# A latent attention stage with its maxima taken in eight portions, its row vectors made by one transposition, and its column sums taken an item later

## The chip, the cores and the metric

The kernel runs on one core of one Trainium2 chip. The metric is device time in microseconds (us) of one execution of the whole program. The core has a matrix engine (TensorE, PE in the profile, with its weight loads as PEld), three engines for elementwise work and reductions (VectorE is DVE, ScalarE is ACT, GpSimd is POOL), and SyncE (SP), which here does nothing but issue transfers between the chip's main memory (DRAM) and the on-chip memory, one after the other. Matmul results land in eight PSUM banks, which this program names bs (three of them), bm (three) and bv (two).

## The reference

One layer over 1024 latent and 256 context tokens of width 1024: a half-step SwiGLU block, two attentions in parallel (neighbourhood attention, and latent attention, MLA, with eight heads), a gated merge, and a second half-step SwiGLU block. The change touches the latent attention alone:

```python
def _attend(q, k, v):
    s = jnp.einsum('bqhd,bkhd->bhqk', q * q.shape[-1] ** -0.5, k).astype(jnp.float32)
    p = jax.nn.softmax(s, axis=-1).astype(v.dtype)
    return jnp.einsum('bhqk,bkhd->bqhd', p, v)
...
q_mla = _mla_q(qn, _axial_rope(qr, ang_r, ang_c))
k_mla = jnp.concatenate([k_ctx_mla, _mla_k(kn, _axial_rope(kr, ang_r, ang_c))], axis=1)
v_mla = jnp.concatenate([cvb, vb], axis=1)
o_mla = _blocked_attention(q_mla, k_mla, v_mla)
```

Each head has 1024 queries and 1280 keys (256 context, 1024 latent). A softmax row needs a shift that is near its maximum, and the sum of its exponentials.

## The kernel before

The work of the latent attention is cut into 16 **items**: item i is head i // 2 and 512 of its queries (the even item the first 512, the odd one the rest). Keys are in ten blocks of 128, two to a step, so an item has five **score steps** p = 0 to 4. A step is ten matmuls: five terms of a product in split precision for each of two key blocks, which sit in the upper and the lower half of the 128 partitions. The scores stand with keys in partitions and queries in columns, so the shift has to be a **row** (one number for each column). It is written as row 32 of each half in the second 512 columns of a query tile (`q[..][1]`, qb below) and enters the scores with the fifth term. ACT then makes the exponentials of both blocks (`Exp`).

Before an item's scores, its shift is made. `maxima` is a generator of **units**: each unit makes coarse scores with queries in partitions, and DVE reduces them to their maxima. An item has five units: four of 512 keys (one for each 128 queries, for both halves of the keys), and a fifth of the remaining 128 keys for all four. `shift` reduces these to four columns of 128 numbers, and `row` turns them into rows: PE multiplies each column, broadcast, with an identity matrix, and ACT copies four pieces of 256 numbers from PSUM into the query tile.

After its scores, an item is **weighed** (`weigh`): 20 matmuls multiply the exponentials with the values, eight matmuls with a column of ones make the column sums (over `l`, in which POOL and DVE have added up the ten blocks), DVE takes their inverses, PE turns these into rows as in `row`, and `out` copies the rows from PSUM, multiplies, and stores both parts of the split result (`heads_out`).

The order is written out by hand in `follow(i, p)`, which is called after score step p of item i. In step 0 it makes the shift of item i + 1 and weighs item i - 1; in the midst of that weighing stands `row` of item i + 1. Units are taken one to a step, so that the fifth unit of item i + 1 comes in step 0 of item i, ahead of the shift. Every engine works through its list in the order of the program.

Loads go through SP, one instruction each, in the order of the program too. The tiles of a head are loaded in four groups: `queries(0)`, ten loads, and the leading keys, six (`leading`, in step 0 of an odd item i, for head i // 2 + 2); then the rest of the keys, eight, and `queries(1)`, ten (`first`), and three loads of values (`second`), both in step 1 of an even item, for head i // 2 + 1. That is 37 loads to a head. An SP instruction that has to wait (for a tile to come free, or for data to store) holds up all that are behind it.

Of the kernel before, what the change touches and what calls it, by code (L numbers as in the profile page):

```python
# [15 lines left out]
P = 128  # L16
# [22 lines left out]
def f32(ap):  # L39
    return ap.bitcast(F32)  # L40
# [3 lines left out]
def hybrid_block(ctx: ExitStack, tc: tile.TileContext, a: dict, out: bass.AP):  # L44
# [1718 lines left out]
    def heads_out(o, free, b, views, cast=False):  # L1763


        for s in range(2):
# [7 lines left out]
            nc.gpsimd.tensor_tensor(lo[b:b + 64], x, f32(hi[b:b + 64]), op=ALU.subtract)  # L1774
# [136 lines left out]
    class MlaHead:  # L1911
# [5 lines left out]
        def leading(self):  # L1917
            self.queries(0)
            self.k1, self.k2 = W(), W()
# [65 lines left out]
    far = []  # L1985

# [6 lines left out]
    max_bank = ["m"]  # L1993
    mla_heads = [MlaHead(h) for h in range(NH)]

    class MlaItem:
# [6 lines left out]
        def maxima(self):  # L2003
# [4 lines left out]
            def products(pb, t, x, keys):  # L2008
# [3 lines left out]
                for u, (q, k) in enumerate(((qa, hd.k1), (qb, hd.k2))):  # L2012
                    for e in range(2):
                        r = slice(64 * e, 64 * e + 64)
                        mmul(pb[e][:, x], q[r, c], k[r, keys], u == 0, u == 1)
                open_group[0] = False

            for t in range(4):
                pb = [PB(max_bank[0]) for _ in range(2)]
                products(pb, t, slice(0, 512), slice(0, 512))  # L2020
                for e in range(2):
                    nc.vector.tensor_reduce(d[:, t, e:e + 1], pb[e], axis=AX.X, op=ALU.max)  # L2022
                yield
            pb = [PB(max_bank[0]) for _ in range(2)]
            for t in range(4):
                products(pb, t, slice(t * P, (t + 1) * P), slice(512, 640))
            for e in range(2):
                nc.vector.tensor_reduce(d[:, :, 2 + e], pb[e].rearrange("p (t c) -> p t c", t=4), axis=AX.X, op=ALU.max)  # L2028
            yield

        def shift(self):


            self.n_ = ST(4)
# [10 lines left out]
        def scores(self, p):  # L2045
            hd = self.hd
            qa, qb = hd.q[self.i % 2]
            pb = [PB("s"), PB("v" if (5 * self.i + p) % 2 else "s")]
            lo, hi, k = slice(0, 512), slice(512, 1024), slice(p * P, (p + 1) * P)
            open_group[0] = True  # L2050
            for u in range(5):
                for e in range(2):
                    r = slice(64 * e, 64 * e + 64)
                    x, y = ((hd.k1[r, k], qa[r, lo]), (hd.k1[r, k], qa[r, hi]), (hd.low_keys(r, p), qa[r, lo]),
                            (hd.k2[r, k], qb[r, lo]), (hd.k3[r, k], qb[r, hi]))[u]
                    mmul(pb[e], x, y, u == 0, u == 4)
            open_group[0] = False
            for e in range(2):
# [3 lines left out]
                nc.scalar.activation(self.part(kb), pb[e], AF.Exp)  # L2062
# [4 lines left out]
        def add(self, kb):  # L2067


            p, n = self.part(kb), 8 if self.i < 14 else 4  # L2070
# [13 lines left out]
        def finish(self):  # L2084
            self.add(8)
            self.add(9)
            nc.vector.tensor_tensor(self.l, self.l, self.acc, op=ALU.add)  # L2087

        def weigh(self):
            self.pv = pv = PB("v")  # L2090
            r, t = ST(4), T2()
            self.rb, self.o = t[:, 0:256], t[:, 256:512]
            for kb in range(10):
                v = self.hd.value(kb)
                x = self.part(kb)
                weigh(pv, 0, (v, v), (x[:, 0:256], x[:, 256:512]), kb == 0, kb == 9)
            for x in range(4):
                weigh(pv, 256 + x, [self.l[:, x * P + 64 * e:x * P + 64 * e + 64] for e in range(2)], (ones, ones), True, True)
            nc.vector.reciprocal(r, pv[:, 256:260])
            if self.i + 2 < 2 * NH:  # L2100
                mla[self.i + 2].row()
            rows_of(pv, 256, r)

        def out(self):
            h, pv, rb, o = self.hd.h, self.pv, self.rb, self.o
            nc.scalar.copy(rb, pv[:, 256:512])
            nc.vector.tensor_tensor(o, pv[:, 0:256], rb, op=ALU.mult)
# [109 lines left out]
    for n in range(len(todo)):  # L2217
# [5 lines left out]
        if n == len(todo) - 3:  # L2223
            max_bank[0] = "s"
            mla_heads[1].leading()
        ahead = chain(start(EARLY), start(AHEAD)) if n == 0 else start(n + AHEAD) if n + AHEAD < len(todo) else top({len(todo) - 3: 2}.get(n, 1))
# [345 lines left out]
```

## Time and profile before

| | |
|---|---|
| time, median of 3 runs | 2552.16 us (2551.08 to 2552.7) |
| the profiled execution | 2552.3 us, span 2550.5 us |
| PE / PEld / DVE / ACT / POOL busy, share of the span | 98% / 81% / 71% / 45% / 12% |
| granted TensorE clock, mean | 0.998 |
| latent attention, first and last exponentials of line 2062 | begin at 1469.5 and 1737.1 us |
| chain that ended last, by engine | PE 87%, ACT 3%, DVE 3%, POOL 3%, DMA 2%, issue 1%, SPq 1% |

A busy PE is read with care: matmuls are pipelined and their ends are modelled. The queue of SP is shown as SPq; its instructions are only the issue of a transfer, and the time to landing runs from the start of the issue until the data is there. Outside the latent attention and the last few items of the neighbourhood attention just ahead of it (nearly nine tenths of the span) the change moves nothing.

### The profile page before, as it was taken

The numbers are of one execution on the slowest core, as the hardware profiler recorded it, in microseconds if no ns is written. First come the engines' busy times: TensorE is split into PE (matmuls) and PEld (weight loads), VectorE is DVE, ScalarE is ACT, GpSimd is POOL, SyncE is SP. The second block draws the span as 40 slices with busy tenths as digits, with TensorE's granted clock in tenths as the row PEclk, the third lists the DMA queues.
The fourth block names the chain that finished last, engine by engine and source line by source line (L and its number), as shares of the span: only waits on it lengthen the run. The fifth ranks groups of instructions, "written<-read, shape, count | busy, mean of one in ns | idle before, by whom it ended". The sixth has DMA issues, their size and how long they took to land.

```text
span 2550.5 us, 39567 instructions
## 1 busy us (share of the span) xinstructions
PE 2502.7 (98%) x14376; PEld 2075.7 (81%) x14376; DVE 1817.2 (71%) x3101; ACT 1145.5 (45%) x2102; POOL 298.8 (12%) x384
## 2 busy tenths in 40 slices
PE   8999999999999999999999999989999999999998
PEld 6888888888898888889887876667888888888887
DVE  4789996887786577874356655556886888766777
ACT  5632233445654753433446744541366323233444
POOL 1000000000000000001002356661021000000003
PEclk9999999999999999999999999999999999999999
DMA  8455543943674566655879764416845445326724
GB/s 308 154 177 191 200 145 120 334 149 136 220 276 144 205 225 215 209 166 174 227 243 246 210 156 119 116 45 241 317 141 197 161 158 164 113 98 239 268 71 165
DMA packets 271877, 474.57 MB, mean 186 GB/s; under 512 B 62658, under 2 KB 96578, under 8 KB 271684
## 3 DMA queue, kind: packets, MB, share of 16 engines
q1 hardware_dynamic: 271684, 472.06, 56.9%
q8 instruction: 113, 1.85, 0.3%
q14 instruction: 80, 0.66, 0.1%
HBM read 355.35 MB, written 116.59 MB: 185 GB/s over the span
## 4 chain that ended last, share of the span: by engine, by line
PE 87%; ACT 3%; DVE 3%; POOL 3%; DMA 2%; issue 1%; SPq 1%; POOLq 0%; DVEq 0%; ACTq 0%
PE bs L157 37%; PE bm L157 29%; PE bv L157 19%; POOL t L2077 2%; PE bm L160 1%; DMA w<-d 1%; SPq L135 1%; DVE t L2087 1%; PE bs L160 1%; ACT t L123 1%; PE bv L160 1%; ACT xp L2062 1%; DVE kr L2028 1%; DVE xu L123 0%; ACT xu L123 0%
## 5 line engine op out<-in xcount | busy, mean ns | idle before, releaser
L123 ACT CAST xu<-t 128x512 fp32r<-128x512 f32 (+1 forms) x270 | 161.0, 601 | 493.9 <-DVE t L123 351.6
L157 PE MATMUL bm<-xu,xu 128*128 128x512 f32 (+2 forms) x1572 | 366.7, 387 | 0.0
L157 PE MATMUL bs<-xv,xu 128*128 128x512 f32 x1488 | 357.3, 389 | 0.3 <-DVE t L123 0.3
L157 PE MATMUL bv<-xv,xu 128*128 128x512 f32 x1342 | 335.4, 389 | 0.0
L157 PEld LDWEIGHTS bm<-xu,xu 128*128 128x128 f32 x1572 | 288.0, 188 | 56.9 <-issue 0.3
L157 PEld LDWEIGHTS bs<-xv,xu 128*128 128x128 f32 x1488 | 279.2, 188 | 58.9 <-issue 1.1
L157 PEld LDWEIGHTS bv<-xv,xu 128*128 128x128 f32 x1342 | 251.9, 188 | 52.2
L157 PE MATMUL bs<-xv,xv 128*128 128x512 f32 x1086 | 265.8, 390 | 0.0
L123 POOL TENSOR_SCALAR st<-st 128x1 f32<-128x1 f32 (+1 forms) x66 | 33.6, 509 | 1883.6 <-ACT t L123 1865.4
L123 DVE TENSOR_TENSOR xu<-xu,xu 128x512 fp32r<-128x512 f32 (+1 forms) x296 | 201.7, 686 | 73.0 <-ACT xu L123 72.5
L157 PEld LDWEIGHTS bs<-xv,xv 128*128 128x128 f32 x1086 | 203.0, 188 | 41.6
L157 PE MATMUL bs<-xu,xu 128*128 128x512 f32 (+1 forms) x972 | 226.1, 381 | 0.0
L123 DVE TENSOR_TENSOR t<-t,t 128x512 f32<-128x512 f32 (+2 forms) x278 | 185.3, 674 | 45.9 <-ACT t L123 36.6
L157 PEld LDWEIGHTS bs<-xu,xu 128*128 128x128 f32 x972 | 177.4, 188 | 35.6 <-issue 1.4
L123 DVE TENSOR_TENSOR xu<-t,xu 128x512 fp32r<-128x512 f32 (+1 forms) x270 | 179.3, 664 | 10.7 <-ACT xu L123 10.6
L157 PE MATMUL bm<-xv,xv 128*128 128x512 f32 x690 | 182.9, 390 | 0.0
L123 ACT CAST xv<-t 128x512 fp32r<-128x512 f32 x170 | 105.7, 622 | 166.9 <-PE bv L157 69.2
L123 ACT CAST xu<-xu 128x512 fp32r<-128x512 f32 x218 | 132.7, 618 | 70.2 <-DMA xu<-in_wo 57.1
L123 DVE TENSOR_TENSOR xv<-t,xv 128x512 fp32r<-128x512 f32 x170 | 117.1, 689 | 64.2 <-ACT xv L123 63.8
L157 PE MATMUL bs<-w,w 64*128 64x512 f32 (+3 forms) x916 | 157.0, 379 | 1.6 <-DVE kr L2022 0.7
L157 PEld LDWEIGHTS bm<-xv,xv 128*128 128x128 f32 x690 | 129.2, 188 | 27.0 <-issue 0.4
L157 PE MATMUL bm<-t,xu 128*128 128x256 f32 x1224 | 147.9, 283 | 0.0
(263 smaller groups left out, 3971.7 us busy)
## 6 DMA issues: line engine op xcount, KB each, us to landing
d<-t SPq DMA_DIRECT2D x350, 256.0 KB, 2.5
t<-d SPq DMA_DIRECT2D x274, 256.0 KB, 3.8
xu<-in_f1w SPq DMA_DIRECT2D x59, 512.0 KB, 4.2
xu<-in_f2w SPq DMA_DIRECT2D x58, 512.0 KB, 3.8
t<-in_wada SPq DMA_DIRECT2D x112, 256.0 KB, 5.0
xv<-in_f1w SPq DMA_DIRECT2D x44, 512.0 KB, 7.4
xu<-in_winT SPq DMA_DIRECT2D x38, 512.0 KB, 4.4
w<-d SPq DMA_DIRECT2D x66, 256.0 KB, 4.7
```

The source lines that it names most:

```text
L123: return lambda *x, **y: pin(f(*x, **y))
L135: return pin(nc.sync.dma_start(dst, src))
L157: return pin(nc.tensor.matmul(o, s, m, start=start, stop=stop, skip_group_check=open_group[0]))
L160: return pin(nc.tensor.transpose(o, x, i))
L2028: nc.vector.tensor_reduce(d[:, :, 2 + e], pb[e].rearrange("p (t c) -> p t c", t=4), axis=AX.X, op=ALU.max)
L2062: nc.scalar.activation(self.part(kb), pb[e], AF.Exp)
L2077: nc.gpsimd.tensor_tensor(self.acc, self.acc, p, op=ALU.add)
L2087: nc.vector.tensor_tensor(self.l, self.l, self.acc, op=ALU.add)
```

## The change

Four things change, all in the latent attention.

1. **Maxima.** An item's maxima come in eight units, each of 128 queries and 320 keys of each half, where there were four of 512 keys and one of four times 128. The units are taken one to a score step, with steps 2 and 4 cut in two for a second one, and one more at the end of step 0: eight to an item. Sixteen units come before item 0, so that those taken in item i are all of item i + 2: its first before the weighing, seven behind.
2. **Rows.** The shift of item i + 1 and the inverse sums of item i - 2 are put side by side into one tile of eight columns. One transposition by PE makes eight rows of them, one ACT copy takes them out of PSUM, and SP carries them on: eight transfers of one row each into the query tile of item i + 1, and, for the inverse sums (of items 0 to 12), one transfer to DRAM and two from there, which repeat a row over 64 partitions each. This is `to_rows`, in step 0.
3. **Column sums.** For items below FAST = 13 the last sum over blocks moves from DVE to POOL and into step 2 of the next item, the column sums and inverses into step 0 of the item behind that, and `out` into step 1 of item i + 4; the weighed values are copied from PSUM at once. Items 13 to 15 keep the way of before.
4. **Loads.** `queries(0)` is issued in step 3 of an even item, the leading keys in step 0 of an odd item behind the transfers of `to_rows`; `first` and `second` stay in step 1 of even items. An early extra `first` of head 1 goes. The low part in `heads_out` moves from POOL to DVE.

```diff
     def to_rows(i, pb):
+        lo, hi = 0 if i + 1 < 2 * NH else 4, 8 if 0 <= i - 3 < FAST else 4
+        turn_(pb[0:hi - lo, 384:512], columns[i][:, lo:hi], ident)
+        rows = T2()
+        nc.scalar.copy(rows[0:hi - lo, 0:P], pb[0:hi - lo, 384:512])
+        if lo == 0:
+            after = mla[i + 1]
+            for e in range(2):
+                for t in range(4):
+                    put(f32(after.hd.q[after.i % 2][1][64 * e + 32:64 * e + 33, 512 + t * P:640 + t * P]), rows[t:t + 1, 0:P])
+        if hi == 8:
+            d = DR([4, P])
+            put(d, rows[4 - lo:8 - lo, 0:P])
+            for x in range(2):
+                put(mla[i - 3].rb[64 * x:64 * x + 64, :],
+                    d.rearrange("t p -> (t p)")[256 * x:256 * x + 256].partition_broadcast(64))
...
             for t in range(4):
-                pb = [PB(max_bank[0]) for _ in range(2)]
-                products(pb, t, slice(0, 512), slice(0, 512))
-                for e in range(2):
-                    nc.vector.tensor_reduce(d[:, t, e:e + 1], pb[e], axis=AX.X, op=ALU.max)
-                yield
...
+                for x in range(2):
+                    pb = [PB(x) for x in next(max_banks)]
+                    products(pb, t, slice(320 * x, 320 * x + 320))
+                    for e in range(2):
+                        nc.vector.tensor_reduce(d[:, t, 2 * x + e:2 * x + e + 1], pb[e][:, 0:320], axis=AX.X, op=ALU.max)
+                    yield
...
-        if after and p == (0 if i else 2):
-            after.shift()
-        if p == 0 and prev:
+        if p == 0:
+            if after:
+                after.shift()
+            if prev:
+                if i > FAST:
+                    prev.total()
+                prev.weigh()
+            pb = prev.pv if prev else PB("v")
+            if 0 <= i - 2 < FAST:
+                mla[i - 2].sums(pb, columns_of(i + 1)[:, 4:8])
+            to_rows(i, pb)
             if i % 2 and i // 2 + 2 < NH:
-                mla_heads[i // 2 + 2].leading()
-            prev.weigh()
...
+                mla_heads[i // 2 + 2].leading_keys()
...
+        if 0 <= i - 4 < FAST - 1 and p == 1:
+            mla[i - 4].out()
...
+        if p == 3 and i % 2 == 0 and i // 2 + 2 < NH:
+            mla_heads[i // 2 + 2].queries(0)
```

**The order on SP.** First the list of before, from the end of one head's `leading` to the `first` of the next. In all these lists a name is a tile with its buffer's number; here w tiles hold queries and keys, and d tensors are in DRAM.

```order
L135 DMA w_16305<-d_381 32x512
L135 DMA w_16305<-d_387 32x512
L135 DMA w_16316<-d_384 64x5x128 x2
L135 DMA w_16317<-d_386 32x5x128 x4
L135 DMA w_16587<-d_386 32x5x128
L135 DMA w_16587<-d_387 32x640
```

All of it is loads from DRAM, with nothing that another engine computes. Now the same place with the change: leading keys of a head (w_15964, w_15965), then `to_rows` of an even item (t_16154 is its ACT copy, t_15689 the tile of the repeated rows), then `first` of that head, down to its second queries (w_16213, w_16214).

```order
L135 DMA w_15964<-d_383 64x5x128 x2
L135 DMA w_15965<-d_386 32x5x128 x4
L135 DMA w_15772<-t_16154 1x16x8 x8
L135 DMA d_16164<-t_16154 4x128
L135 DMA t_15689<-d_16164 64x256 x2
L135 DMA w_16204<-d_386 32x5x128
L135 DMA w_16204<-d_387 32x640
```

Eleven transfers that come from the ACT copy of this item stand between the leading keys and the rest of the head's loads; the second queries come eight loads further down, and the next head's leading keys stand behind eleven more (of t_16392).

**The order on PE in step 0 of an item.** Before, from the last product of the fifth unit on (bm_16914): weighing into bv_16935, column sums (strip holds the ones), rows of the shift (bm_16967), rows of the inverse sums.

```order
L157 MATMUL bm_16914<-w_16317,w_16597 128x128
L157 MATMUL bv_16935<-xp_16698,w_16165 64x256 x10
L157 MATMUL bv_16935<-xp_16835,w_16165 64x256 x2
L157 MATMUL bv_16935<-xp_16835,w_15895 64x256 x4
L157 MATMUL bv_16935<-xp_16835,y_12989 64x256 x4
L157 MATMUL bv_16935<-strip,t_16910 64x1 x8
L157 MATMUL bm_16967<-ident,st_16933 64x128 x4
L157 MATMUL bv_16935<-ident,st_16936 64x128 x4
```

With the change, in the odd item that follows the SP list above, from the last score products of step 0 on:

```order
L157 MATMUL bv_16333<-w_15772,w_15762 128x512
L157 MATMUL bm_16349<-w_15964,w_16213 128x320
L157 MATMUL bm_16350<-w_15964,w_16213 128x320
L157 MATMUL bm_16349<-w_15965,w_16214 128x320
L157 MATMUL bm_16350<-w_15965,w_16214 128x320
L157 MATMUL bv_16358<-xp_16106,w_15762 64x256 x10
L157 MATMUL bv_16358<-xp_16251,w_15762 64x256 x2
L157 MATMUL bv_16358<-xp_16251,w_15532 64x256 x4
L157 MATMUL bv_16358<-xp_16251,y_12989 64x256 x4
L157 MATMUL bv_16358<-strip,t_16109 64x1 x8
L160 MATMUL bv_16358<-ident,st_16143 8x128
```

Both groups of rows have given way to one transposition at the end. The unit ahead of the weighing is now the first unit of item i + 2, and it reads the second queries (w_16213, w_16214) that the SP list above loads.

More of the change, by code (lines that the diff above doesn't have):

```diff
@@ L2282, in follow @@
                 item.add(kb)
-    UNITS0, UNITS = (2, 2, 1, 1, 1), (1, 1, 1, 1, 1)
     for i, item in enumerate(mla):
         for p in range(5):
-            item.scores(p)
-            if i and p == 0:
-                mla[i - 1].finish()
-            for _ in range((UNITS if i else UNITS0)[p]):
+            for lo, hi in ((0, 2), (2, 5)) if p in (2, 4) else ((0, 5),):
+                item.scores(p, lo, hi)
+                if i and p == 0:
+                    mla[i - 1].finish()
                 next(tops, None)
```

104 lines of the change are left out of this document (64 added, 40 removed).

## The prediction

> **What bounds the kernel now.** I read the page first, then the stage's windows, its waits, and the timelines of one item on PE, DVE and SP. The reciprocal of the column sums runs once an item, so its line gives the length of an item (first and last start, in us):
>
> ```profile
> L2099 DVE RECIPROCAL st<-bv x14: 172/173/174, 1490.7 to 1713.3; 128x4 f32<-128x4 f32 x14
> 1490.70:1713.40 222.70, 201.66 (x2002) 152.28 (x2002) 127.45 (x198) 107.67 (x235) 139.64 (x117) 0.99 0.43 108
> PEld bv L157 <- DVE t L2087: 16.5, 13, 1.4
> PE bv L157 <- DVE t L2087: 10.6, 13, 1.0
> PE bm L157 <- DVE st L2035: 9.7, 13, 0.8
> ```
>
> Thirteen items take 222.6 us: 17.1 each, **34.2 a pair**. The window (length, then busy PE, PEld, DVE, ACT, POOL) has PE idle for 21.0 us. The waits (us in total, times, longest) name nearly all of that: 10.6 for the column sums' last addition and 9.7 for the shift, 1.6 an item. No wait of PE is for a transfer. One item on PE (start, us, idle before):
>
> ```profile
> 1602.73 1.23 PE L157 MATMUL bm<-w,w 64*128 64x128 f32 x16
> 1603.89 3.67 PE L157 MATMUL bv<-xp,w 128*64 128x256 f32 x32
> 1607.39 1.03 PE L157 MATMUL bv<-xp,y 128*64 128x256 f32 x8
> 1609.35 0.63 PE L157 MATMUL bv<-strip,t 128*64 128x1 f32 x16 [0.93 <-DVE t L2087]
> 1610.76 0.66 PE L157 MATMUL bm<-ident,st 128*64 128x128 f32 x8 [0.77 <-DVE st L2035]
> 1611.24 0.61 PE L157 MATMUL bv<-ident,st 128*64 128x128 f32 x8
> 1611.78 0.49 PE L157 MATMUL bs<-w,w 64*128 64x512 f32 x1
> ```
>
> The fifth unit takes 1.16, weighing 4.5 (to 1608.4), sums 0.63, the two groups of rows 0.48 and 0.54, and two stalls stand between. That is what the change works on. SP in the same stretch, and the landing of its loads (median, by size):
>
> ```profile
> 1600.88 12.17 SPq L135 DMA_DIRECT2D w<-d  x20
> 1613.10 0.47 SPq L135 DMA_DIRECT2D y<-d  x1
> 1613.66 9.79 SPq L135 DMA_DIRECT2D w<-d  x16
> w<-d SPq DMA_DIRECT2D x119, 64.0 KB, 3.1
> w<-d SPq DMA_DIRECT2D x48, 80.0 KB, 2.5
> SPq L135 <- PE bs L157: 47.1, 6, 12.3
> ```
>
> A head's 37 loads take 22.6 us, **0.61 a load**, of the 34.2 that a pair lasts; SP then waits up to 12.3 us for tiles that PE still reads. It is free for a third of the time, and early.
>
> **The change, part by part.** *On PE alone it saves.* Stalls 1.6; two groups of rows 1.0. A unit of 320 keys is four matmuls in two pairs; of 512 columns:
>
> ```profile
> 1600.92 0.39 PE L157 MATMUL bs<-w,w 64*128 64x512 f32 x1
> 1601.14 0.39 PE L157 MATMUL bv<-w,w 64*128 64x512 f32 x1
> 1601.15 0.84 PE L157 MATMUL bm<-w,w 64*128 64x512 f32 x4
> 1601.60 1.52 PE L157 MATMUL bs<-w,w 64*128 64x512 f32 x10
> ```
>
> So a pair of 512 columns takes 0.23 (1600.92 to 1601.15), a unit of two 0.45 (to 1601.60), ten score matmuls 1.13 (to 1602.73), and a pair of 128 takes 1.16/8 = 0.145. For 320 I take 0.15: eight units 2.4, against 4 x 0.45 + 1.16 = 2.97. Against these 3.2 us stand the transposition (0.2) and a reciprocal now bare, 0.3, since no rows cover it: 2.7 saved an item, about 14.4 left.
>
> *DVE* gets 16 reductions for ten. Two of 512 take 1.29, below; by size a reduction of 320 takes 0.41, by count 0.64: 6.6 to 10.3 an item, beside some 3.5 of other work. That is under 14.4, so I take nothing; without that cover the slower count would make items of 13.8, still no bound.
>
> ```profile
> 1601.80 1.29 DVE L2022 TENSOR_REDUCE kr<-bm 128x1 f32<-128x512 f32 x2 [0.30 <-PE bm L157]
> L2077 POOL TENSOR_TENSOR t<-t,xp 128x512 f32<-128x512 f32 x78 | 105.2, 1349 | 6.8 <-ACT xp L2062 1.8
> L1774 POOL TENSOR_TENSOR xo<-t,xo 64x256 fp32r<-64x256 f32 x26 | 19.0, 732 | 76.2 <-ACT xo L1773 75.7
> L2042 ACT CAST w<-bm 1x256 fp32r<-1x256 f32 x52 | 18.8, 362 | 93.7 <-PE bm L157 93.2
> ```
>
> *POOL* gets the sum of two accumulators, 1.35, and loses the low parts, 2 x 0.73 (on DVE among the 3.5): 8 x 1.35 = 10.8 an item, and a whole item until it is read. *ACT* loses four copies of 0.36 and gets one. Neither is near 14.4: nothing. The early extra `first` of head 1 was 18 loads that nobody waited for: nothing.
>
> *SP is where it costs.* `to_rows` puts eleven transfers on it that wait for this item's PE and ACT, and the loads of the next heads queue behind them. Nearest rows for the short ones, stores of 1 and 32 rows elsewhere in the program, and of 128 KB:
>
> ```profile
> 1230.58 1.40 SPq L135 DMA_DIRECT2D d<-t  x4
> d<-t SPq DMA_DIRECT2D x2, 64.0 KB, 1.6
> d<-t SPq DMA_DIRECT2D x26, 128.0 KB, 1.8
> d<-t SPq DMA_DIRECT2D x350, 256.0 KB, 2.5
> ```
>
> A row costs between 0.36 (1.40 + 0.05 over four) and 0.61. I take 0.45, nearer to the stores, which also start on chip: 8 x 0.45 = 3.6. The store to DRAM must land before the two that read it can go: 1.6 to 2.5, taken 1.8; these two 0.36 to 0.61 each, taken 1.1 together. So **x = 6.5 us** of SP per item, from 2.9 + 1.6 + 0.7 = 5.2 to 4.9 + 2.5 + 1.2 = 8.6. No row here can make x zero.
>
> Now a pair of items, from T, the end of the even item's ACT copy. PE does the rest of that item (a second unit, four steps of 1.13, six units, small gaps: 7.1) and the next item's step 0 scores (1.2), and, 0.3 ahead of ACT, stands at the unit before the weighing at T + 8.0. That unit reads `queries(1)`. On SP these stand behind x and eight loads: 6.5 + 8 x 0.61 + 5 x 0.61 to the sixth load's issue, + 3.1 to land = T + 17.6. **PE waits 9.6 us.** From there to the next ACT copy: unit 0.3, weighing 4.5, sums 0.6, reciprocal 0.3, transposition and copy 0.4: 6.1, so T' = T + 23.7. SP meanwhile has 31 loads (18 of `first`, 3, and `queries(0)` of the next head) behind x: free at 6.5 + 18.9 = T + 25.4, later than T'. Then x again, and the six leading keys: 25.4 + 6.5 + 3.1 + 2.5 to land = T + 37.5. PE, at the next even item's first unit since T' + 8.0 = 31.7, **waits 5.8 us** for them. T'' = 37.5 + 6.1 = T + 43.6. In general a pair is 30.6 + 2x: **9.4 us more than 34.2**. The saving on PE is spent in these waits.
>
> The whole stage: units ahead of item 0 cost 16 x 0.3 - (6 x 0.45 + 1.16) = 0.9, and item 0 begins where its first exponentials were, 1469.5; its ACT copy comes some 2 us on, at 1472.4. Items 0 to 2 have no inverse rows, so 3.6 for x: to the copy of item 2, 3.6 + 18.9 + 3.6 + 3.1 + 2.5 + 6.1 = 37.8; on to item 4, 22.5 + 6.5 + 3.1 + 2.5 + 6.1 = 40.7; four pairs to item 12, 174.4; to item 13, which waits only for the last `queries(1)`, 23.7. That is 1749.0. Before, PE was at this place at 1697.4:
>
> ```profile
> 1469.47 1.09 ACT L2062 ACTIVATE xp<-bs 128x512 f32<-128x512 f32 x2 [0.65 <-PE bs L157]
> 1697.42 0.96 PE L157 MATMUL bs<-w,w 64*128 64x512 f32 x6
> 1524.00:1528.00 4.00, 3.38 (x24) 2.81 (x26) 0.93 (x4) 1.82 (x5) 0.00 (x0) 0.57 0.66 173
> ```
>
> So +51.6; the last items have no such waits and give back about 2 (one item's stalls and a little): +49.6. One more term: right after two stalls (of 0.9 and 0.8) PE was once granted a clock of 0.57 for 4 us (window above), 0.43 x 4 = 1.7 us lost. The change has 13 waits, all longer. Between 0 and 22 us; it came once in 13 items, but after far shorter gaps, so I take 9. **Sum: 2552.3 (the profiled execution, 0.1 above the median) + 49.6 + 9 = 2611 us.**
>
> **Rivals.** *PE sets the pace (faster).* Were loads and rows in time, 13 items would each save 2.7, less 2 for the ends: 2552.3 - 33 = 2519. For it: SP is free for a third of the time now, and the loads overlap well. Against it: `queries(1)` has 8.0 us from T, and even with x = 0 its loads need 13 x 0.61 + 3.1 = 11.0. A pair breaks even at x = 1.8; eleven issues at the cheapest row, 0.36, are 4.0. It needs issue to be twice as quick as any row of this stage has it. *The clock stays low.* If every wait is followed by two stretches such as the one shown, 13 x 3.4 = 44 in place of 9: 2646. For it speak the lengths, 9.6 and 5.8; against it that the shown stretch was short. [...] *The change doesn't do what it says*, in that the sums or the shift still end late: the sums then cost 0.9 an item inside a block that already waits, and the time moves by 12 us at most, to 2623, which my range holds. *No change*: SP's wait just eats the saving, x = 1.8, 2552.
>
> **How the numbers follow.** Forecast 0.72; low clock 0.15; PE sets the pace 0.08; near no change 0.05 (of this 0.02 within 0.2%, 0.02 slower, 0.01 faster). The forecast's own range: x = 5.2 takes off 1.3 for each of ten full sets of transfers and 0.7 for the three short ones, 15, and the clock 9: 2587; x = 8.6 adds 10 x 2.1 + 3 x 1.3 = 25, the clock 13: 2649. To hold 8 in 10 with shorter landings on quieter queues, I let it begin at 2576, and end at 2646, where low clock and long transfers meet. Measurement tells 0.2% (5 us) from nothing. Faster 0.09, same 0.02, slower 0.89.
>
> **What would show it.** Right: PE's waits for DVE (the sums, the shift) gone; in their place waits of bm matmuls in step 0 for transfers into w, about 9 us in odd and 6 in even items; PE's idle time in the stage up from 21 to well over 100 us; items alternating, a pair near 43; SP issuing nearly without pause; granted clock below 1 behind the waits. Wrong: short issues of rows (under 0.2), a pair under 34, or PE waiting for DVE's reductions.

## The result, and the profile after

The changed kernel takes **2671.7 us** (median of 4 runs, 2668.1 to 2672.9) against 2552.4 for the kernel before in the same measurement (2551.1 to 2553.3): a ratio of **1.0465, 95% interval 1.0447 to 1.0484**. That is 119 us slower; forecast were 59 us, with a range to 2646. The sign and the mechanism were right, the size was not: the measured time lies 61 us above the forecast and 26 above the range's end.

The profiled execution has a span of 2670.7 us and a mean granted clock of 0.975 (before 0.998). On the page, the slices of the latent attention now show PE idle and its clock lowered (rows of slices, PE and granted clock; the stage fills slices 23 to 28):

```profile
PE   8999999999999999999999777778999999999998
PEclk9999999999999999999999878879999999999999
```

First the waits of the stage (engine and line, then what was waited for: us in total, times, longest):

```profile
PEld bm L157 <- DVE kr L2062: 44.3, 34, 6.2
PE bm L157 <- DMA w<-d: 42.6, 33, 6.3
DVE t L2147 <- DMA t<-d: 39.3, 13, 6.1
PE bm L157 <- DVE kr L2062: 33.2, 9, 5.8
PE bv L157 <- ACT t L2137: 6.8, 12, 0.6
```

Before, none of PE's waits here was for a transfer. Now 42.6 us are for loads of queries and keys (tiles w), as forecast. But 33.2 are for DVE's reductions, and DVE in turn waits 39.3 us in 13 waits for the transfers that repeat the inverse rows (t from DRAM). That was not in the forecast.

SP's list from the copy of an even item on, which starts at T = 1622.50 (start, us from the first to the last of the group, number):

```profile
1622.78 4.98 SPq L135 DMA_DIRECT2D w<-t  x8
1627.80 0.47 SPq L135 DMA_DIRECT2D d<-t  x1
1629.31 1.13 SPq L135 DMA_DIRECT2D t<-d  x2
1630.54 11.78 SPq L135 DMA_DIRECT2D w<-d  x20
1642.95 5.81 SPq L135 DMA_DIRECT2D w<-d  x10
1652.01 0.57 SPq L135 DMA_DIRECT2D w<-t  x1
```

Eight row transfers of 512 bytes take SP 4.98 us, 0.62 each: as long as a load of 64 to 256 KB (0.59 in the mean of the twenty above, 0.61 before). With the store, the wait for its landing (1629.31 - 1627.80) and the two repeating transfers, x is 1622.78 to 1630.5, **7.7 us**, within the bounds of 5.2 to 8.6 but above the 6.5 taken. At 1648.8 SP is through with these loads, and it stands for 3.3 us until the next copy, whose row transfers begin at 1652.01. So here the pace is not set by SP's own work alone: whatever delays that copy delays the next row transfers. PE meanwhile (start, us, idle before, from that item into step 0 of the next, an odd one):

```profile
1633.67 0.90 PE L157 MATMUL bm<-w,w 64*128 64x320 f32 x3 [5.22 <-DVE kr L2062]
...
1639.65 0.38 PE L157 MATMUL bm<-w,w 64*128 64x320 f32 x1 [1.34 <-DMA w<-d]
1641.48 1.21 PE L157 MATMUL bm<-w,w 64*128 64x320 f32 x3 [1.45 <-DMA w<-d]
1642.61 6.40 PE L157 MATMUL bv<-xp,w 128*64 128x256 f32 x32
1648.85 1.03 PE L157 MATMUL bv<-xp,y 128*64 128x256 f32 x8
1650.44 0.63 PE L157 MATMUL bv<-strip,t 128*64 128x1 f32 x16 [0.57 <-ACT t L2137]
```

The last load that the unit needs is there at 1641.48 = T + 19.0, or 18.7 from the end of the copy, where the forecast counts from and has 17.6. Part of the wait before it shows as a wait for DVE (5.22), the rest as waits for DMA. Then weighing takes 7.27 us, from 1642.61 to 1649.88, in place of 4.54. The granted clock says why (window, length, busy PE, PEld, DVE, ACT, POOL, then **granted clock**, DMA share, GB/s):

```profile
1635.00:1636.00 1.00, 1.00 (x9) 0.85 (x8) 0.79 (x2) 0.38 (x1) 0.00 (x0) 0.50 0.47 136
1638.30:1641.50 3.20, 0.41 (x3) 0.23 (x2) 0.00 (x0) 1.04 (x2) 2.17 (x2) 0.97 0.85 206
1641.50:1643.00 1.50, 1.50 (x5) 0.94 (x7) 0.76 (x2) 0.00 (x0) 0.00 (x0) 0.50 0.48 115
1647.00:1648.00 1.00, 1.00 (x8) 0.62 (x6) 0.00 (x0) 0.00 (x0) 0.00 (x0) 0.50 0.87 264
```

The clock is at half behind the wait for DVE, and at half again for 6.5 us from 1641.5 to 1648, through the weighing, on which the next copy and so the next row transfers wait. How often that happens is seen in the groups by line (busy us, mean ns of one) of the 13 weighings of items 0 to 12, the kernel before first, the changed one behind the dots:

```profile
L157 PE MATMUL bv<-xp,w 128*64 128x256 f32 x416 | 47.8, 382 | 0.0
...
L157 PE MATMUL bv<-xp,w 128*64 128x256 f32 x416 | 75.8, 544 | 0.0
```

The same 416 matmuls take **28.0 us more**. The pair of items, between starts of even items' copies (the windows' bounds), stands at 51.2 to 53.3 us, against 34.2 before and 43.6 forecast:

```profile
1571.28:1622.50 51.22, 37.32 (x280) 26.53 (x281) 20.91 (x44) 14.44 (x31) 20.93 (x16) 0.83 0.32 79
1622.50:1651.73 29.23, 20.31 (x141) 14.52 (x141) 9.53 (x22) 7.16 (x15) 10.18 (x8) 0.77 0.44 111
1651.73:1675.80 24.07, 18.60 (x141) 12.70 (x141) 11.04 (x22) 7.28 (x15) 10.69 (x8) 0.86 0.15 34
1727.65:1779.50 51.85, 37.66 (x280) 26.60 (x282) 21.42 (x44) 14.47 (x31) 20.91 (x16) 0.84 0.32 79
```

The four pairs from 1571.28 to 1779.48 take 208.2, **52.05** each: from the even item's copy to the odd one's 29.2 here (forecast 23.7), on to the next even one's 24.1 here and 22 to 24 in all (forecast 19.9).

### The profile page after: what moved, and what is told of

It is laid out like the page before. It is cut to its first block, busy times and chain, and to the rows that moved or that the text cites. A ratio compares the mean times of both kernels' runs of the same rounds, so it can differ in the third digit from the quotient of the medians.

```text
span 2670.7 us, 39477 instructions
## 1 busy us (share of the span) xinstructions
PE 2551.5 (96%) x14168; PEld 2098.1 (79%) x14168; DVE 1831.2 (69%) x3216; ACT 1130.9 (42%) x2058; POOL 287.8 (11%) x365
## 3 DMA queue, kind: packets, MB, share of 16 engines
q1 hardware_dynamic: 275884, 472.16, 54.8%
## 4 chain that ended last, share of the span: by engine, by line
PE 90%; DMA 4%; SPq 2%; ACT 2%; DVE 1%; issue 1%; POOL 0%; DVEq 0%; POOLq 0%; ACTq 0%
PE bs L157 36%; PE bm L157 29%; PE bv L157 22%; SPq L135 2%; DMA w<-d 2%; PE bm L160 1%; PE bv L160 1%; PE bs L160 1%; DMA t<-d 1%; ACT t L123 1%; DMA d<-t 0%; DVE xu L123 0%; DVE t L123 0%; ACT xv L123 0%; DVE xv L123 0%
## 5 line engine op out<-in xcount | busy, mean ns | idle before, releaser
L157 PE MATMUL bm<-w,w 64*128 64x320 f32 (+1 forms) x572 | 116.8, 358 | 84.4 <-DMA w<-d 43.1
L157 PE MATMUL bs<-w,w 64*128 64x512 f32 (+3 forms) x918 | 170.9, 392 | 0.5 <-DVE xp L1786 0.4
L157 PEld LDWEIGHTS bm<-w,w 64*128 64x128 f32 x572 | 76.4, 198 | 115.2 <-DVE kr L2062 45.5
L2062 DVE TENSOR_REDUCE kr<-bm 128x1 f32<-128x320 f32 x241 | 108.1, 486 | 81.0 <-PE bm L157 75.3
```

The lines of the kernel that those rows point to most:

```text
L157: return pin(nc.tensor.matmul(o, s, m, start=start, stop=stop, skip_group_check=open_group[0]))
L2062: nc.vector.tensor_reduce(d[:, t, 2 * x + e:2 * x + e + 1], pb[e][:, 0:320], axis=AX.X, op=ALU.max)
```

## The experiments

Three theories were put against each other. **Theory 1**: SP's list sets the pace (row transfers, then loads, then the unit, then weighing, then the next row transfers). **Theory 2**: DVE's list does (reductions stand behind the multiplication by the inverse rows, which waits for its transfer). **Theory 3** concerns the low clock: it costs on the path, or it is hidden under the landings. All edits are of the changed kernel unless said otherwise. The ratios are to the kernel before, run beside.

### Does SP's list set the pace?

**rows_twice**: the cost under suspicion doubled.

```diff
-                for t in range(4):
+                for t in (0, 1, 2, 3, 0, 1, 2, 3):
                     put(f32(after.hd.q[...][1][64 * e + 32:64 * e + 33, 512 + t * P:640 + t * P]), rows[t:t + 1, 0:P])
```

> Each of the eight row transfers of the shift is issued twice (the same bytes to the same place), so x, SP's time in this step per item, grows by 8 x 0.63 = 5.0 us. Theory 1 (pair = constant + 2x): a pair is 10 us longer, over 6.5 pairs 65, time 2730 to 2745. Rival (the transfers run beside other waits and don't set the pace): below 2690.

Measured 2741.9 us, ratio 1.0753 (1.0731 to 1.0774), 70 us more than the changed kernel. The row transfers of an item in SP's list (as above, 4.98 there):

```profile
1654.00 10.04 SPq L135 DMA_DIRECT2D w<-t  x16
```

The 5.06 us that SP spends more per item come back in full: a pair takes 62 us in place of 52. This is theory 1's "constant + 2x".

**row_pe**: the eight shift rows off SP, the inverse rows still through DRAM.

```diff
-        lo, hi = 0 if i + 1 < 2 * NH else 4, 8 if 0 <= i - 3 < FAST else 4
+        lo, hi = 4, 8 if 0 <= i - 3 < FAST else 4
...
+        if p == 1 and after:
+            after.row()
```

> The shift rows go by TensorE and four ACT copies again, as in the kernel before, but in step 1; the inverse rows still go by transposition, DRAM and two repeating transfers. So eight of the eleven row transfers per item leave SP, about 5.0 us of 7.7. Theory 1: a pair is 2 x 5.0 shorter, 41.5 in place of 51.5, and the time falls by 6.5 x 10 = 65 less about 8 for the rows on PE, to 2600 to 2625; it stays slower than the kernel before. Rival (the transposition and copy block or the eight portions cost the time, not the transfers): 2660 or more.

Measured 2584.1 us, ratio 1.0133 (1.0103 to 1.0162): 88 us less than the changed kernel, more than the 47 to 72 expected. The clock is lowered less behind the shorter waits (1.8 us at most, below; mean 0.995 against 0.975): the 16 weighings take 63.8 us here and 87.3 in the changed kernel, which is most of the surplus. What is left of PE's waits in the stage:

```profile
PE bm L157 <- DVE kr L2062: 11.6, 16, 1.3
PE bm L157 <- DMA w<-d: 11.1, 10, 1.8
```

**unit_behind**: the unit that needs the newly loaded tiles put behind the weighing and the ACT copy, and nothing else.

```diff
-                next(tops, None)
+                if p or not i:
+                    next(tops, None)
...
-            if p == 0:
-                next(tops, None)
+            for _ in range((2 if i else 1) * (p == 0)):
+                next(tops, None)
```

> The unit of step 0 that reads queries or keys is put behind the weighing, the transposition and the ACT copy of that step, so that the next row transfers no longer wait for it; nothing else is changed. Theory 1: the loop from row transfers over loads, unit, weighing and back to row transfers is cut; what is left is SP's own time, 37 x 0.6 + 2 x 7.7 = 38 us a pair, and the shift rows that queue behind the loads: pair of 40 to 44 in place of 51.5, time 2600 to 2630. Theory 2 (DVE's order sets the pace): units wait as before, time within 10 of 2672.

Measured 2604.9 us (two runs, 2599.7 and 2610.1), ratio 1.0215 (1.0166 to 1.0264), pairs of some 41: 67 us gained without one transfer less. So more than half of the loss is the loop's. The other 52 us stay, and with them the transfers: the expectation put SP's own time at 38 us a pair. There is still a wait of 3.7 to 5.8 us for DVE in even items, and the clock falls to 0.50 around it, but now in front of units and score steps; from item 5 on weighing is at full clock again (PE's instructions, start, us, idle before; behind the dots two windows, granted clock third from the end):

```profile
1607.86 0.90 PE L157 MATMUL bm<-w,w 64*128 64x320 f32 x3 [5.82 <-DVE kr L2062]
1612.61 3.67 PE L157 MATMUL bv<-xp,w 128*64 128x256 f32 x32
...
1611.00:1612.00 1.00, 1.00 (x7) 0.98 (x5) 0.97 (x3) 0.00 (x0) 0.00 (x0) 0.50 0.92 137
1613.00:1614.00 1.00, 1.00 (x14) 0.64 (x12) 0.00 (x0) 0.62 (x2) 0.71 (x2) 1.00 0.26 84
```

**rows_act**: ACT issues the eight row transfers, SP the rest.

```diff
-                    put(f32(after.hd.q[...]...), rows[t:t + 1, 0:P])
+                    pin(nc.scalar.dma_start(f32(after.hd.q[...]...), rows[t:t + 1, 0:P]))
```

> The eight row transfers of the shift are issued by ACT, right behind its copy, in place of SP; the DRAM store and the two repeating transfers stay on SP. Theory 1: x on SP falls from 7.7 to about 2.7, as in row_pe, so that the time falls to 2584 or so, plus what ACT's 8 issues cost: 4 to 5 us of ACT an item ahead of the exponentials of step 1, some 3 of which PE waits for where it has no other wait: 2585 to 2625. Rival (each short transfer costs the DMA queues, whoever issues it): 2660 or more.

Measured 2626.9 us, ratio 1.0302 (1.0282 to 1.0323), 2 us above the upper end of theory 1. ACT now spends the 5 us, and its exponentials wait behind them; PE waits 31.9 us for these (ACT's list in one item, then a row of PE's waits):

```profile
1622.08 5.00 ACTq L2025 DMA_DIRECT2D w<-t  x8
1627.13 1.57 ACT L2099 ACTIVATE xp<-bs 128x512 f32<-128x512 f32 x3 [5.08 <-DMA w<-t]
...
PE bs L157 <- ACT xp L2099: 31.9, 15, 3.2
```

So on both lists a transfer of 512 bytes cost its issuer 0.62 (4.98 and 5.00 for eight); here one can choose the list, not avoid the price.

### Does DVE's list set the pace?

**out_late**: the multiplication three steps later in the code.

```diff
-        if 0 <= i - 4 < FAST - 1 and p == 1:
+        if 0 <= i - 4 < FAST - 1 and p == 4:
             mla[i - 4].out()
```

> The multiplication by the repeated inverse rows (line 2147) is put three steps later in the item, from step 1 to step 4, so that reductions no longer queue behind it on DVE while it waits for its transfer. Theory 1 (SP's order sets the pace: weighing waits for a unit, the unit waits for queries or keys that stand behind the row transfers on SP): PE's waits for DVE inside the item, 3 to 6 us each, go, and its wait for the transfer in step 0 grows by as much; pair of items near 51 as in the changed kernel, time 2660 to 2680. Theory 2 (DVE's order sets the pace: the units wait for reductions that stand behind the multiplication): 13 waits of about 4.4 us go, 57 us, time near 2615.

Measured 2671.8 us, ratio 1.0477 (1.0447 to 1.0507): no change, but the run says nothing of theory 2. DVE's first multiplications stand where they stood; the changed kernel, then behind the dots this run:

```profile
1559.45 1.02 DVE L2147 TENSOR_TENSOR t<-t 128x256 f32<-128x256 f32 x1 [0.31 <-DMA t<-d]
1570.73 0.18 DVE L2142 RECIPROCAL st<-bv 128x4 f32<-128x4 f32 x1 [6.53 <-PE bv L157]
...
1559.39 1.12 DVE L2147 TENSOR_TENSOR t<-t 128x256 f32<-128x256 f32 x1 [0.20 <-DMA t<-d]
1572.22 0.18 DVE L2142 RECIPROCAL st<-bv 128x4 f32<-128x4 f32 x1 [7.85 <-PE bv L157]
```

In both the first multiplication comes before the reciprocal of item 4's step 0, although the code writes it behind, in step 1 or step 4. The description of the kernel above has to be corrected here: PE and SP work in the program's order, but in this stage the instructions of DVE, ACT and POOL are not held in it, and a scheduler puts the multiplication into the item ahead, right behind its own transfers. A second correction bears on this: the inverse sums that `to_rows` carries in item i are those of item i - 3, not i - 2, so that the first of them go out in item 3.

**out_pinned**: reductions and multiplication held in the written order.

```diff
-                        nc.vector.tensor_reduce(d[:, t, ...], pb[e][:, 0:320], axis=AX.X, op=ALU.max)
+                        pin(nc.vector.tensor_reduce(d[:, t, ...], pb[e][:, 0:320], axis=AX.X, op=ALU.max))
...
-                nc.vector.tensor_tensor(o, o, rb, op=ALU.mult)
+                pin(nc.vector.tensor_tensor(o, o, rb, op=ALU.mult))
```

> In the run with the later multiplication (out_late) DVE's list came out as before the edit: in this stage DVE's instructions are placed by the scheduler, not by the program's order. Here the reductions of the units and the multiplication by the inverse rows are held in the written order, which puts the multiplication four reductions behind the NEXT item's reciprocal, a whole item after its transfers. Theory 1 (SP's order sets the pace): PE's waits of 3 to 6 us for DVE go, its waits for transfers in step 0 grow by as much, pair near 51, time 2660 to 2680. Theory 2 (DVE's order sets the pace): 13 waits of about 4.4 us go, time near 2615.

Measured 2658.8 us, ratio 1.0424 (1.0403 to 1.0445): 13 us less than the changed kernel, not 57. PE's wait in step 0 turns into one for the transfer:

```profile
1686.15 0.60 PE L157 MATMUL bm<-w,w 64*128 64x320 f32 x1 [5.18 <-DMA w<-d]
1688.06 1.26 PE L157 MATMUL bm<-w,w 64*128 64x320 f32 x3 [1.30 <-DMA w<-d]
1689.24 6.28 PE L157 MATMUL bv<-xp,w 128*64 128x256 f32 x32
```

The waits for DVE lay in front of a wait for SP and were covered by it; theory 2 falls as the pace, and keeps 13 us: one bare wait near the end (below), and weighings at full clock (4.54) in the even items, where one wait is gone.

### What does the low clock cost?

Here PE is given products that nobody reads, written to the bank which the weighing then overwrites.

```diff
+        def busy(self, n):
+            self.pv = PB("v")
+            v, x = self.hd.value(0), self.part(0)
+            for _ in range(n):
+                weigh(self.pv, 0, (v, v), (x[:, 0:256], x[:, 256:512]), True, True)
...
                 if i and p == 0:
                     mla[i - 1].finish()
+                    if i < 14:
+                        mla[i - 1].busy(20 if i % 2 else 11)
                 next(tops, None)
```

**fill_late** has this beside the edit of out_late:

> As the run with the later multiplication, and in step 0 of each item, ahead of the unit that waits for queries or keys, PE is given products that nobody reads (20 or 11 steps of weighing of 0.45 us, written to the bank that weighing then overwrites), so that it stays busy while the transfer is under way. Theory 1 with the clock (each wait is followed by a weighing at a low clock, 5.7 to 7.3 us in place of 4.5, and this loss lies on the path because the next row transfers wait for that weighing): the weighings return to about 4.5, and the time falls by 14 x 2 to 14 x 3, to 2630 to 2645 although PE does about 90 us more work. Theory 3 (the clock in the waits doesn't matter, only the landing does): weighing stays near 6.6 or the gain is lost elsewhere, 2665 to 2690.

Measured 2679.3 us, ratio 1.0507 (1.0472 to 1.0541). All weighings of these items were at 4.54, as the clock theory has it, but in odd items the products ended some 5 us after the landing, so the gain went into them.

**fill_pinned** (beside the edit of out_pinned, `busy(20 if i % 2 else 10)`) and **fill_short** (`busy(13 if i % 2 else 5)`):

> As out_pinned, and PE is given 20 or 10 steps of products that nobody reads (0.45 us each) in step 0 ahead of the unit that waits, so that it is busy until about the landing (T + 19 in odd, + 14 in even items). Theory 1 with the clock: every weighing at 4.5 us in place of 4.5 to 7.3, the waiting unit at 0.3 to 0.5 in place of 1.1; blocks of 6.6 us in place of 7.9 to 8.9; pair 47 to 48, time 2640 to 2650. Theory 3 (the low clock in the waits costs nothing, only landings count): time as out_pinned or up to 15 above it.

> As fill_pinned, with 13 and 5 steps of products that nobody reads in place of 20 and 10: in fill_pinned they ended 3 and 2 us after the landing, and the clock's gain went into that. They should now end with the landing. Theory 1 with the clock: weighing 4.54 in every item; from the ACT copy to the next weighing about 19.5 in odd and 14.5 in even items, blocks 6.4; pair near 47, time 2625 to 2640, against 2658.8 without the products. Theory 3 (the low clock costs nothing): 2655 to 2665.

Measured 2663.8 us (1.0444, 1.0423 to 1.0464) and 2653.7 us (1.0407, 1.0386 to 1.0428): neither fell to the 2625 to 2650 expected. In the first the products again outlasted the landing by 3 and 2 us; in the second they ended too early in most odd items, and two waits of 1.2 and 1.8 brought back weighings of 6.2 us. **fill_odd** has `busy(17 if i % 2 else 0)`:

> As out_pinned, with 17 steps of products that nobody reads in odd items only (13 ended too early in fill_short, and two waits of 1.2 and 1.8 and a slow weighing of 6.2 followed; 20 ended too late). Even items have weighings of 4.54 without them. If the slow weighing lies on the path: odd items' weighing 4.54, next copy at T + 27.5 in place of T + 30, pair 48.2 in place of 50.6, time 2640 to 2648. If it does not (the time is set by landings alone): 2655 to 2662.

Measured 2651.8 us, ratio 1.0396 (1.0377 to 1.0415), **7 us** less than out_pinned. The intervals of the two ratios just overlap, so that the traces have to decide. In the later pairs it does what was expected: behind the 68 products come, with no wait, the unit and a weighing at full clock (start, us; of the weighing the first 32 matmuls):

```profile
1679.63 7.56 PE L157 MATMUL bv<-xp,w 128*64 128x256 f32 x68
1688.08 3.67 PE L157 MATMUL bv<-xp,w 128*64 128x256 f32 x32
```

The last two full pairs take 48.1 in place of 50.6. Of the two before, one was not slow in out_pinned either, and in the other the slow weighing moved on to the even item; nothing is gained there. So in these pairs the loss is on the path, about 2.5 us for a weighing of 7 us. Together the two edits, out_pinned and fill_odd, win 20 us back out of the changed kernel. How much of that is clock and how much the removed waits themselves the runs don't separate.

### What are the parts worth without the transfers?

**portions**: of the change, the eight portions of 320 keys with their order of units, and the low parts on DVE. The sums, inverse rows and shift rows go as before.

```diff
-    FAST = 13
+    FAST = -1
...
     def to_rows(i, pb):
+        return
...
             nc.vector.reciprocal(r, pb[:, 256:260])
+            if self.i + 2 < 2 * NH:
+                mla[self.i + 2].row()
...
```

> Only the eight portions of 320 keys are left of the change (with the order of units that comes with them): column sums, inverse rows and shift rows go as in the kernel before, in the same item and by TensorE. By the prediction's own prices PE saves 2.97 - 2.40 = 0.57 an item, 8 to 9 us in all, and DVE's 16 reductions lie under PE's work: 2540 to 2548. Rival: the reductions, 3 us more of DVE per item, push the shift and the last addition of the sums, for which PE waits 1.6 us an item, further back: 2555 to 2580.

Measured **2543.7 us**, ratio 0.9974 (0.9962 to 0.9986). The size is as forecast; PE's waits, however, are now for reductions:

```profile
PE bm L157 <- DVE kr L2062: 22.9, 17, 1.6
```

**rows_pe** and **rows_step1**: late sums too, and all rows by TensorE. In rows_pe the inverse rows go into the weighing's bank, sums and shift rows into a bank of their own in step 1:

```diff
     def to_rows(i, pb):
+        if 0 <= i - 3 < FAST and i < len(mla):
+            rows_of(pb, 256, columns[i][:, 4:8])
+            nc.scalar.copy(mla[i - 3].rb, pb[:, 256:512])
...
+        if p == 1 and (after or 0 <= i - 2 < FAST):
+            pt = PB("m")
+            if 0 <= i - 2 < FAST:
+                mla[i - 2].sums(pt, columns_of(i + 1)[:, 4:8])
+            if after:
+                after.row(pt)
```

In rows_step1 (diff against rows_pe) the sums follow the weighing, ahead of ACT's copy of that bank, and all rows come in step 1:

```diff
-            to_rows(i, pb)
+            if 0 <= i - 2 < FAST:
+                mla[i - 2].sums(pb, columns_of(i + 1)[:, 4:8])
+            if prev and i <= FAST:
+                nc.scalar.copy(prev.o, pb[:, 0:256])
...
-        if p == 1 and (after or 0 <= i - 2 < FAST):
...
+        if p == 1 and (after or 0 <= i - 3 < FAST and i < len(mla)):
+            to_rows(i, PB("m"))
```

> All of the change but its transposition and transfers: eight portions, column sums two items later, multiplication four items later; the rows of the inverse sums and of the shift are made on TensorE from columns and copied by ACT, the shift's in step 1. No short transfers on SP, so no waits of PE for loads. By the prediction's prices PE saves 1.6 (stalls) + 0.57 (portions) = 2.2 an item, and pays a copy of the weighed sums on ACT: 2552 - 14 x 2.2 = 2521, between 2515 and 2535, faster than the kernel before. Rival (the later sums and portions themselves cost, through DVE's list or the banks): 2545 or more.

> As rows_pe, with the column sums back behind the weighing, in its bank, ahead of ACT's copy of that bank, and the rows of the inverse sums and of the shift together in step 1, in a bank of their own, so that no write to a bank stands behind a read of the same bank by ACT or DVE (in rows_pe PE waited 0.47 and 1.07 an item there). Neither waits for a value of the same step. If those two waits were all that took rows_pe's gain: 1.5 x 13 = 20 off 2553.5, 2525 to 2538, faster than the kernel before and than the portions alone. Rival (the waits move on to other banks or to ACT's copies): 2543 or more.

Measured 2553.5 us (1.0013, 1.0003 to 1.0022) and 2549.8 us (0.9998, 0.9989 to 1.0008): both rivals, no gain. The waits moved, in rows_pe to the reciprocal and to ACT's copy of a bank that PE wants to write on, in rows_step1 to the reductions (rows_pe, then rows_step1):

```profile
PE bm L157 <- DVE st L2128: 13.5, 13, 1.1
PE bv L157 <- ACT t L2123: 5.2, 11, 0.5
...
PE bm L157 <- DVE kr L2051: 18.3, 15, 1.6
```

What stood on DVE ahead of those reductions was line 1774, the low parts that the change moved there from POOL; in rows_step1 (the line's instructions: shortest, median, longest in ns) up to 1.5 us:

```profile
L1774 DVE TENSOR_TENSOR xo<-t,xo x28: 416/763/1493, 1531.2 to 1736.9; 64x256 fp32r<-64x256 f32 x28
```

**portions_low**, **step1_low**, **after_low**: this line back on POOL, in the portions alone, in rows_step1 and in the changed kernel.

```diff
-            (nc.vector if cast else nc.gpsimd).tensor_tensor(lo[b:b + 64], x, f32(hi[b:b + 64]), op=ALU.subtract)
+            nc.gpsimd.tensor_tensor(lo[b:b + 64], x, f32(hi[b:b + 64]), op=ALU.subtract)
```

> As the portions alone, with the low parts (line 1774) back on POOL, where the kernel before has them. In the run with the portions alone PE waits 1.35 us an item for a reduction that stands on DVE behind these subtractions, which cost DVE 0.41 each and 0.49 of waiting for ACT's cast. If the step 'DVE's added work lies under PE's' failed by that edit: 14 x 1.0 to 1.35 less, 2525 to 2532, clearly below 2543.7 and below the kernel before. Rival (the sixteen reductions themselves fill DVE, or POOL's 1.5 us an item make the last addition late): 2538 to 2550.

> As rows_step1, with the low parts (line 1774) back on POOL. There these subtractions take DVE 0.88 us each, and PE waits 18.3 us in 15 waits for reductions behind them. If that is the cause: 2549.8 - 13 x 1.2 to 1.4, 2531 to 2536. Rival (reductions and ACT's copies bound the item at 16.9): 2543 or more.

> The changed kernel with the low parts (line 1774) back on POOL, nothing else. Theory 1 (transfers set the pace; what DVE does beside lies under PE's waits): 2662 to 2674. Rival (DVE's list is part of the 119 us lost): 2650 or less.

Measured 2538.6 us (0.9953, 0.9940 to 0.9965), **2536.4 us (0.9945, 0.9931 to 0.9958)** and 2673.9 us (1.0482, 1.0463 to 1.0502). In the first the gain is 5 us (the intervals touch), not the 12 to 19 expected, and the time in the rival's range: of the waits for reductions 1.8 us are left, but the last addition of the sums is waited for again. In the second it is 13, at the edge of what was expected. In the changed kernel it is nothing, as theory 1 has it: there this work of DVE's lies under waits for transfers. PE's waits in portions_low, then in step1_low:

```profile
PE bv L157 <- DVE t L2126: 10.0, 13, 1.2
PE bm L157 <- DVE kr L2062: 1.8, 4, 0.9
...
PE bm L157 <- DVE kr L2051: 3.7, 6, 1.8
```

step1_low is faster than both kernels by 14 and 135 us. Between it and portions_low the intervals overlap, so that no gain of the late sums beside the portions is shown. Why the subtraction of line 1774 takes 0.42 at the median in portions and 0.76 in rows_step1 was not tried.

## Why the prediction was wrong in size

By its steps:

- **"x = 6.5 us of SP per item"**: mis-sized, 7.7 in the item shown and 8.0 in the mean of items 3 to 12 (7.7 to 8.7); the short sets of items 0 to 2 took 5.6 to 6.1 where 3.6 was taken. The row transfers cost 0.62 where 0.45 was taken; the stores of 1 and 32 rows (0.36) were the wrong neighbours, the loads (0.61) the right one. The two repeats, 1.13, came as taken, and the store landed in 1.5 where 1.8 was taken. That x enters a pair twice is shown by rows_twice.
- **"PE waits 9.6 us" (odd), "5.8 us" (even)**: the landings came 18.7 us after the even copy, not 17.6, and 13.6 after the odd one (the keys were there at 1665.6), where the forecast has 13.8. The second agreement is luck: the forecast has SP still busy with loads for 1.7 us behind the odd copy, but SP had been through for 3.3 us, and a longer x took up the difference. So the sign "SP issuing nearly without pause" did not come: in the pair shown SP stands 3.3 us before the odd copy and 11.6 before the next even one. Nor did PE's idle time reach "well over 100 us": it is 91, from 1490 to 1865. That the wait shows in two parts, one of them under DVE's name, was not foreseen. The list named "PE waiting for DVE's reductions" as a sign against the forecast; out_pinned and after_low show that it was not one, except once: at the end of item 13, where no load stands between it and the next weighing, the wait is bare.

```profile
1819.85 0.90 PE L157 MATMUL bm<-w,w 64*128 64x320 f32 x3 [5.18 <-DVE kr L2062]
```

- **"6.1" from the unit to the next copy**: at full clock 0.3 + 6.4 (4.54 weighing, 1.85 to the copy), 0.6 too little. The missing piece is the wait of 0.57 of the column sums for ACT's copy of the weighed values (6.8 us in 12 waits, above): sums and values share a bank. In rows_step1, where the sums stand ahead of that copy, PE has no such wait.
- **"Between 0 and 22 us ... I take 9" for the clock**: **this is the step that failed**, with the price of the row transfers beside it. Weighing alone lost 28.0 us (the two groups above), and both the value and its upper bound were too low. That this loss lies on the path is read from SP, which stands waiting for the copy behind the weighing, and tried by fill_odd. The bound came from one stretch of 4 us at 0.57. The trace has longer ones: 6.5 us of work at 0.50 behind the waits of step 0, 4.7 in unit_behind (from 1607.8 to some 1612.5). The rival "the clock stays low" (2646, chance 0.15) had the right mechanism with 44 us for 13 waits; the 28.0 lie between. How long a wait has to be for such a stretch to follow, and what ends it, no run shows.
- **"PE saves 2.7 an item"**: this saving was spent in the waits, as forecast. Where no transfers wait, the portions' share is confirmed by the portions alone (7 us of 8 to 9). The share of the stalls is not: rows_pe, expected to gain 31 us, and rows_step1 gained nothing, and step1_low gained 14.
- **"DVE: I take nothing"**: right for the low parts in the changed kernel (after_low, no difference), wrong as a rule: in rows_step1 the same work costs 13 us, and in the portions alone PE waits 22.9 us for reductions.
- **"The last items give back about 2"**: wrong. From the last copy that the forecast timed to the end it lost some 9: the kernel before took from 1697.4 to its last reciprocal at 1743.1, 45.7; the changed one from 1808.7 to 1863.5, 54.8. The bare wait is 5.2 of it.

```profile
L2099 DVE RECIPROCAL st<-bv x16: 172/173/184, 1490.7 to 1743.1; 128x4 f32<-128x4 f32 x16
L2142 DVE RECIPROCAL st<-bv x16: 182/183/183, 1521.6 to 1863.5; 128x4 f32<-128x4 f32 x16
```

The sum again with what was measured: 2602 without any clock term (2552.3 + 49.6); to the copy of item 13 59.7 more (1808.7 against 1749.0), of which 28.0 are slow weighings, 6.6 the wait in the shared bank, 2.3 a later start, and the 23 left over a longer way from copy to weighing; and 11 at the end (9 lost, 2 not given back). That makes 2672.7, the time of the profiled execution (2672.9); it has to, since the 23 are a remainder. By the forecast's own rule the longer x makes 22 of them (ten full sets at 1.5 more, three short ones at 2.3 more). So of the 61 us that the forecast lacked, the clock in the weighings makes 19 (28.0 where 9 were taken), the row transfers some 22, the end 11, the bank 6.6 and the start 2.3: no term alone would have brought the forecast to the measured time. The 28 are read from the trace; that such a loss lies on the path is shown by fill_odd, but only for the odd items' part of it.

## What to carry to other kernels

A short transfer cost its issuer as much here as a long one (0.62 for 512 bytes, 0.61 in the mean for loads of 64 to 256 KB). Before replacing engine work by transfers, count them on the list that issues them, and look for a loop: here row transfers held up loads, loads a unit, the unit a weighing, and the weighing the next row transfers; putting the unit behind the weighing, with the same transfers, took 67 of the 119 us back.

A wait of PE cost twice here, by its length and by the clock behind it (0.50 for 4.7 to 6.5 us of work in the stretches shown); price the work that follows a wait at the clock that the trace shows there, and put into that place work on which nothing waits. And look at each part of a change by itself: here the portions alone were good for 12 us once a side edit, the low parts on DVE, was taken back, and the late sums with rows by TensorE added nothing clear of noise (14).

## What was not expected of the hardware

- Two waits of 1.34 and 1.45 us with 0.4 us of work between them, in a stretch that had a clock of 0.97 again after the longer wait ahead of it, were followed by a clock of 0.50 over the next 6.5 us; behind two waits of 1.2 and 1.8 in fill_short a weighing took 6.2 in place of 4.54.
- Moving the multiplication by three steps in the code moved nothing on DVE (it starts at 1559.39 in out_late, at 1559.45 without), while PE and SP keep the written order here (unit_behind's weighing at 1612.61 follows the score steps without a unit between; the 16 row transfers of rows_twice stand in a row at 1654.00). Which engines' lists follow the code has to be read from the lists.
- The issue of a transfer of 512 bytes took 0.62 us on SP (4.98 for eight) and 0.62 on ACT (5.00), and a store of four rows 0.47; the stores of 1 and 32 rows elsewhere in this program had taken 0.36 in the mean.
